# Four edits to a decoder layer's small products: the value sums' turn, the new tokens' scores, the running sums and the inner norms

## The chip, the cores and the metric

The kernel runs on one core of one Trainium2 chip. A core has TensorE (PE: matrix products, with weights loaded by a second queue, PEld), VectorE (DVE), ScalarE (ACT), GpSimd (POOL) and SyncE (SP), which issues most of the transfers. Every engine takes its instructions in the order of its own list and waits for the others on semaphores. SBUF is the working memory with 128 partitions, PSUM holds the results of products in eight banks. The metric is the device time of one execution in microseconds (us).

## The reference

One step of a decoder with one layer on two groups of tokens at once: a prompt of 256 tokens, and 8 sequences of 4 new tokens each (32 tokens) with a past of 1024 tokens in pages of 128 rows. All inputs are float32.

```python
hp = ffn_half(hp, norm_ffn1, w_ffn1_gate, w_ffn1_up, w_ffn1_down)   # h + 1/2 * (silu(n@wg) * (n@wu)) @ wd
cb, u, q, k, v, logf = mixer_in(hp, norm_mix, w_in, b_f)             # one projection, log sigmoid of 8 gates
conv_y = cb * short_conv(u_ext, conv_w)
attn_o = fox_prompt(q, k, v, logf)        # new tokens: fox_sample(..., cache_k, cache_v, cache_logf, page_table)
hp = mixer_out(hp, conv_y, attn_o, norm_conv_out, norm_attn_out, w_out)  # each group normalised by itself
hp = ffn_half(hp, norm_ffn2, ...)
hp = ple_add(hp, p_prompt, norm_ple, w_ple_gate, w_ple_proj)
y_prompt = rms_norm(hp, norm_final)
```

and for the new tokens

```python
F = jnp.cumsum(lf_all, axis=1).transpose(0, 2, 1)       # running sum of log forget values, past and new
s = jnp.einsum('bqhd,bkhd->bhqk', q, k_all) * SCALE
s = s + Fq[..., None] - F[:, :, None, :]                # Fq: the running sums at the new tokens
s = jnp.where(kpos <= qpos, s, -jnp.inf)
return jnp.einsum('bhqk,bkhd->bqhd', jax.nn.softmax(s, axis=-1), v_all)
```

`rms_norm(x, g)` is `x * rsqrt(mean(x*x) + 1e-6) * g`. D_MODEL is 2048, D_FF 5632, there are 8 heads of 128, and the page table says which pages of the pool a sequence has.

## The kernel before

Everything is held with features on the partitions and the 288 tokens (256 prompt, 32 new) in the free dimension: `h` is 128 x 16 x 288. Weights come as float32 pieces of 512 by 256 (`wraw`, 512 KB). For accuracy each operand is split into a high part in float32r and the rest: `whi` (ACT, line 271) and `wlo` (DVE, line 272) of the weights, `xh` and `xl` of the activations. Three products give one: `whi*xh`, `whi*xl`, `wlo*xh` (lines 304 to 306). `pair` (line 282) makes two output blocks of 128 features of such products; a piece of weights is a chunk of it, 4 k-tiles x 2 blocks x 3 = 24 products, and its splits are made up to five half pieces ahead (`HALVES`).

The program is one list of steps that is written out in order: first feed-forward, mixer, second feed-forward, per-layer embedding, final norm. Small work goes between the chunks in two ways. `defer(fn, n)` (line 334) puts a function off by n chunks; `run_deferred` calls what is due in the middle of a chunk, after its first block's 12 products. In the mixer, `at(i, ...)` (line 952) puts functions ahead of the i-th chunk of the filling work, and functions at one mark run in the order in which they were added. From this list the framework plans each engine's own order when the kernel is built, by its estimate of when operands are ready, with the order of the program as priority; a few instructions are pinned (`keep_in_program_order`).

What the change touches:

- **Inner norms.** The squares of `h` are added up over the 16 k-tiles in `acc` (line 209). `norm_scale` (line 190) defers `inv_rms` (line 175) by 1 to 3 chunks. That sums over the partitions by a product of the 128 x 128 constant `mean` (1/2048 everywhere) with the squares, in float32 (line 180), then makes the inverse root with two activations on ACT and three operations on DVE. It is called six times: at the eighth chunk for the first norm (line 444, two chunks), at the end of each feed-forward (line 397, three), for the convolution's group (line 999, two), the attention's group (line 1000, one), and at the end of the mixer (line 1006, three). The final norm calls `inv_rms` by itself (line 1066).
- **Running sums.** `f_past` (line 530) scans the log forget values of the 64 pages and keeps each page's total per head in `tot` (64 x 8). `f_natural` (line 555) turns those of the new tokens to rows (`nat`, columns 32 to 40). `f_new`, `f_turn` and `f_rows` (lines 566 to 595), each a chunk after the one before, add up totals and new values per new token by two products (lines 568, 569), turn the result (line 576), spread it over the 128 rows of (head, sequence, half, token) by a product (line 583), and make from it the bias `newbias` of the new tokens' scores and the running sum at each query, `Fq`.
- **New tokens' scores.** The keys of the past come by 16 key units (`k_scores`, line 667), one at every third mark from 1, each 16 products in column tiles of 32 (line 684). Eight units make the scores of four sequences, a group. `new_scores` (line 695) makes the scores among the new tokens of a group, 16 short products in the same column tiles (line 699), at marks 20 and 21; `softmax(0)` is at mark 27.
- **Value sums.** `v_round` (line 733) takes a page of values of each of the four sequences; after the eighth round `sample_out` (line 750) takes the heads' diagonal blocks out of PSUM into `so`, eight operations of DVE (lines 762 and 764), and defers `sample_turn` (line 767) by two chunks, which turns `so` (line 770) and puts it into `oS` (line 772). The second group's turn then stores the values and normalises. The first group's `sample_out` is at mark 69, as is the first of the eight `prompt_head` calls (line 784); two of the chunks behind carry the gated convolution's evacuations (line 848).

Of the kernel before, what the change touches and what calls it, by code (L numbers as in the profile page):

```python
# [16 lines left out]
F32 = mybir.dt.float32  # L17
F32R = mybir.dt.float32r
I32 = mybir.dt.int32
AF = mybir.ActivationFunctionType  # L20
ALU = mybir.AluOpType
# [4 lines left out]
P = 128  # L26
D = 2048
# [3 lines left out]
DT = 4  # L31
NS = DB * DT
NT = SEQ + NS
DFF = 5632
NH = 8
# [26 lines left out]
def constants():  # L62

    rows = np.arange(P)
    hc, b, half, t = rows // 32, rows % 32 // 8, rows % 8 // 4, rows % 4
    h = 4 * half + hc
    parts = []

    def put(name, a):
        a = np.asarray(a, np.float32)  # L70
        full = np.zeros((P, a.shape[1]), np.float32)
        full[: a.shape[0]] = a
        at = sum(x.shape[1] for x in parts)
        CONST_COLS[name] = (a.shape[0], at, at + a.shape[1])
        parts.append(full)

    put("ident", np.eye(P))
    put("ones", np.ones((P, 1)))
    put("mean", np.full((P, P), 1.0 / D))
    put("iota", rows[:, None])  # L80
    put("headmask", (rows % 8 // 4 * 4 + rows % 32 // 8)[:, None] == np.arange(NH)[None])
    put("tri", np.where(np.arange(P)[None] <= rows[:, None], 0.0, NEG))
    cb, ct = np.arange(NS) // DT, np.arange(NS) % DT
    for g in range(2):
        own = (cb[None] == (b + 4 * g)[:, None])
        put(f"newmask{g}", np.where(own & (ct[None] <= t[:, None]), 0.0, NEG))
        put(f"newself{g}", own & (ct[None] == t[:, None]))
    put("fold", rows[:, None] % 32 == np.arange(NH)[None])
    put("tri32", (cb[:, None] == cb[None]) & (ct[:, None] <= ct[None]))
    pb, pg = np.arange(64) // PAGES, np.arange(64) % PAGES  # L90
    put("tri64", (pb[:, None] == pb[None]) & (pg[:, None] < pg[None]))
    put("sel64", pb[:, None] == cb[None])
    put("headsel", np.arange(NH)[:, None] == h[None])
    return np.concatenate(parts, 1)


def build(nc, tc, ctx, A, O):
# [3 lines left out]
    v, s, g, pe, sy = nc.vector, nc.scalar, nc.gpsimd, nc.tensor, nc.sync  # L101

    cst = pool("cst")
# [14 lines left out]
    def ktbank():  # L118

        names = [n for n in spare["tags"] for _ in range(BANKS[n])]  # L120
        spare["at"] += 1
        n = names[spare["at"] % len(names)]
        return bank(n, BANKS[n])
# [3 lines left out]
    h = cst.tile([P, KT, NT], F32, name="h")  # L127

    def const(name):
        r, a, b = CONST_COLS[name]  # L130
        return C[:r, a:b]

    ident = const("ident")
# [5 lines left out]
    at = 0  # L139
# [32 lines left out]
    def log_tables():  # L172
        tc.keep_in_program_order(s.preload_act_table_set("natural_log_exp_and_others"))

    def inv_rms(out, parts, width, load=True):

        b = ktbank()
        m = b[:, :NT]
        for i, x in enumerate(parts):
            pe.matmul(m, const("mean"), x, start=i == 0, stop=i == len(parts) - 1)  # L180
        if load:
            log_tables()
        c = float(D // width)
        s.activation(ra, m, AF.Ln, bias=eps, scale=c)
        s.activation(out, ra, AF.Exp, scale=-0.5)
        v.scalar_tensor_tensor(ra, out, -0.5 * c, out, ALU.mult, ALU.mult)
        v.scalar_tensor_tensor(ra, m, EPS / c, ra, ALU.add, ALU.mult)
        v.scalar_tensor_tensor(out, ra, 1.5, out, ALU.add, ALU.mult)

    def norm_scale(out, squares, width, chunks):  # L190

        defer(lambda: inv_rms(out, [squares], width), chunks)

    def split(hi, lo, x, gcol):
        return (s.activation(hi, x, AF.Copy, scale=gcol),
# [138 lines left out]
    def defer(fn, chunks=1):  # L334

        deferred.append((state["chunk"] + chunks, fn))
# [218 lines left out]
    def f_natural(lf, FT):  # L555
        fp = W["fp"][0]
        np_ = ktbank()
        nat = cst.tile([P, 40], F32, name="nat")
        for j in range(2):
            pe.transpose(np_[:, 16 + j * NH:16 + j * NH + NH], FT[:, j * P:j * P + P], ident[:NH, :NH])  # L560
        pe.transpose(np_[:NS, 32:40], lf[:, SEQ:], ident[:NH, :NH])
        v.tensor_copy(nat[:, 16:32], np_[:, 16:32])
        v.tensor_copy(nat[:NS, 32:40], np_[:NS, 32:40])
        M["nat"] = nat

        def f_new():
            pn = ktbank()
            pe.matmul(pn[:NS, :NH], const("tri32"), nat[:NS, 32:40], start=True, stop=False)
            pe.matmul(pn[:NS, :NH], const("sel64"), M["tot"], start=False, stop=True)
            Fn = fp.tile([NS, NH], F32, name="Fn")  # L570
            v.tensor_copy(Fn, pn[:NS, :NH])
            defer(lambda: f_turn(Fn))

        def f_turn(Fn):
            pt = ktbank()
            pe.transpose(pt[:NH, :NS], Fn, ident[:NS, :NS])
            FnT = fp.tile([NH, NS], F32, name="FnT")
            v.tensor_copy(FnT, pt[:NH, :NS])
            defer(lambda: f_rows(FnT))

        def f_rows(FnT):
            px = ktbank()
            pe.matmul(px[:, :NS], const("headsel"), FnT, start=True, stop=True)
            Fx = fp.tile([P, NS], F32, name="Fx")
            v.tensor_copy(Fx, px[:, :NS])
            M["newbias"], M["Fq"] = [], []
            for gi in range(2):
                nb = cst.tile([P, NS], F32, name=f"nbias{gi}")
                v.tensor_tensor(nb, const(f"newmask{gi}"), Fx, ALU.subtract)
                d = fp.tile([P, NS], F32, name=f"fd{gi}")  # L590
                v.tensor_tensor(d, Fx, const(f"newself{gi}"), ALU.mult)
                fq = cst.tile([P, 1], F32, name=f"fq{gi}")
                v.tensor_reduce(fq, d, AX.X, ALU.add)
                M["newbias"].append(nb)
                M["Fq"].append(fq)

        defer(f_new)
# [97 lines left out]
    def new_scores(gi):  # L695
        sc = ktbank()
        for half in range(2):
            for c in range(4):
                pe.matmul(sc[32 * c:32 * c + 32, :NS], M["qn"][gi][:, 4 * half + c, :], k_[4 * half + c][:, SEQ:],
                          start=half == 0, stop=half == 1, tile_position=(0, 32 * c))  # L700
        v.scalar_tensor_tensor(M["s", gi][:, PAGES * P:], sc[:, :NS], M["Fq"][gi], M["newbias"][gi], ALU.add, ALU.add)
# [48 lines left out]
    def sample_out(gi):  # L750
        mx = W["vv"][0]
        for b in range(4):
            for e in range(2):
                rows = slice(NS * e, NS * e + NS)
                pe.matmul(M["va", gi][e][32 * b:32 * b + 32, :], M["pv", gi][rows, 8, b], M["vs"][rows], start=False, stop=True,
                          tile_position=(NS * e, 32 * b))
        o = mx.tile([P, P], F32, name="so", tag="so", bufs=2)
        for hh in range(NH):
            src = M["va", gi][hh // 4][:, hh % 4 * P:hh % 4 * P + P]
            m = const("headmask")[:, hh:hh + 1]  # L760
            if hh == 0:
                v.tensor_scalar(o, src, m, None, ALU.mult)
            else:
                v.scalar_tensor_tensor(o, src, m, o, ALU.mult, ALU.add)
        defer(lambda: sample_turn(gi, o), 2)

    def sample_turn(gi, o):
        mx = W["vv"][0]
        t = ktbank()
        pe.transpose(t[:, :P], o, ident)  # L770
        for half in range(2):
            v.tensor_copy(M["oS"][:, 4 * half:4 * half + 4, 16 * gi:16 * gi + 16].rearrange("p c (b t) -> p c b t", t=DT),
                          t[:, :P].rearrange("p (b c a t) -> p a c b t", c=4, a=2, t=DT)[:, half])
        if gi == 1:
            s.dma_start(O["v_prompt"].rearrange("(j p) c -> p j c", p=P), M["vn"])
            for e in range(2):
                s.dma_start(O["v_sample"][:, 512 * e:512 * e + 512], M["vs"][NS * e:NS * e + NS])
            for hh in range(NH):
                split(za[hh][0][:, SEQ:], za[hh][1][:, SEQ:], M["oS"][:, hh, :], gain("norm_attn_out", hh))
            sq = mx.tile([P, NH, NS], F32, name="sqS")  # L780
            s.activation(sq, M["oS"], AF.Square)
            v.tensor_reduce(acc[:, SEQ:], sq.rearrange("p h n -> p n h"), AX.X, ALU.add)
# [169 lines left out]
    def at(i, *fns):  # L952
        marks.setdefault(i, []).extend(fns)
# [31 lines left out]
        fill += pair(A["w_out"], ob * 256, list(range(8)), lambda k: zc[k], out_conv(ob), late=1 if ob == 0 else 0)  # L985
    for n in range(16):
        at(1 + KSTEP * n, units[n] if n > 1 else units[n][1])
    at(20, lambda: new_scores(0))
    at(21, lambda: new_scores(1))
    at(27, lambda: softmax(0))  # L990
    at(49, lambda: softmax(1))
    at(48, v_start)
# [144 lines left out]
```

## Time and profile before

| | |
|---|---|
| median of 3 runs | 2333.52 us (2333.39 to 2333.70) |
| span of the profiled execution, first to last instruction | 2332.0 us |
| time of the profiled execution itself | not listed apart from the three; the runs lie 1.4 to 1.7 us above the span |
| mean granted TensorE clock | 0.998 |
| busy: PE, PEld, DVE, ACT, POOL | 99%, 97%, 57%, 45%, 14% of the span |
| read from and written to HBM | 435.56 MB, 5.07 MB |

How to read the rows: in a group of instructions (a line that begins with a line number) stand the line, the engine, the operation, output <- inputs, shapes and the number of instructions, then busy time and mean ns of one, then the idle time of the engine just before them and what ended it. In a timeline stand the start and the duration in us, the engine, the line, the operation, the tiles, how many were merged, and in brackets an idle time of the engine before it. In the chain of waits stand a start, a length, and what the time went to. A product in float32 appears as two instructions (x2), one in float32r as one. In the view of waits stand the waiting instruction, what it waited for, the total in us, the number and the longest.

### The profile page before, as it was taken

The page shows a single profiled execution, that of the slowest core. Times are in us where ns is not written, and L with a number is a line of the kernel's source. Part 1 is how long each engine was busy: PE and PEld are TensorE (multiplying, and loading weights), DVE is VectorE, ACT ScalarE, POOL GpSimd, SP SyncE. Part 2 cuts the span into 40 slices and gives each one's busy share as a digit, 9 for nine tenths or more (in the row PEclk, how much of TensorE's full clock was granted, in tenths as well). Part 3 has the DMA queues.
Part 4 walks back from the last instruction along what each step waited for, and adds up shares of the span by engine and source line. Part 5 has one row for each costly group of instructions (what it writes and reads, how often), then busy time and mean ns, then how long its engine had stood idle before and what let it go on. Part 6 is the DMA issues. An engine that isn't in the chain of part 4 may idle for free.

```text
span 2332.0 us, 44271 instructions
## 1 busy us (share of the span) xinstructions
PE 2316.4 (99%) x17390; PEld 2254.6 (97%) x17390; DVE 1338.6 (57%) x2395; ACT 1056.0 (45%) x1859; POOL 328.2 (14%) x401
## 2 busy tenths in 40 slices
PE   9999999999999999999999999999999999999997
PEld 9999999999999999888888999999999999999997
DVE  6555555555555575456466765555555555555755
ACT  7444444444444453334345554444434444444654
POOL 2010000000000013444445210000000000000110
PEclk9999999999999999999999999999999999999999
DMA  8575555545555457998988554545555555555452
GB/s 272 162 241 163 165 169 164 164 164 167 167 163 163 163 161 224 333 313 268 322 306 296 167 165 154 174 158 175 163 164 164 170 163 163 164 167 167 161 169 88
DMA packets 391137, 443.52 MB, mean 190 GB/s; under 512 B 17120, under 2 KB 371824, under 8 KB 390928
## 3 DMA queue, kind: packets, MB, share of 16 engines
q1 hardware_dynamic: 369456, 366.89, 49.3%
q0 software_dynamic: 20384, 71.38, 8.8%
q8 instruction: 136, 2.23, 0.4%
q10 hardware_dynamic: 1088, 2.42, 0.3%
q14 instruction: 73, 0.60, 0.1%
HBM read 435.56 MB, written 5.07 MB: 189 GB/s over the span
## 4 chain that ended last, share of the span: by engine, by line
PE 99%; DVE 0%; DMA 0%; ACT 0%; SPq 0%; issue 0%; DVEq 0%
PE mm L304 31%; PE mm L306 31%; PE mm L305 30%; PE va L742 1%; PE va L684 1%; PE va L304 1%; PE va L306 1%; PE va L305 1%; DMA h<-in_x_dram 0%; DVE h L1072 0%; PE kt L304 0%; PE kt L306 0%; PE kt L305 0%; PE kt L180 0%; PE kt L796 0%; PE kt L829 0%
## 5 line engine op out<-in xcount | busy, mean ns | idle before, releaser
L272 DVE TENSOR_TENSOR wlo<-wraw,whi 128x512 fp32r<-128x512 f32 x1384 | 972.0, 706 | 805.2 <-ACT whi L271 753.2
L271 ACT ACTIVATE whi<-wraw 128x512 fp32r<-128x512 f32 x1384 | 865.3, 630 | 938.5 <-PE mm L305 866.0
L304 PE MATMUL mm<-xh,whi 128*128 128x288 f32 x3680 | 1094.9, 298 | 0.0
L305 PE MATMUL mm<-xl,whi 128*128 128x288 f32 x3680 | 1085.6, 295 | 0.0
L306 PE MATMUL mm<-xh,wlo 128*128 128x288 f32 x3680 | 1082.0, 294 | 0.0
L304 PEld LDWEIGHTS mm<-xh,whi 128*128 128x128 f32 x3680 | 689.7, 187 | 23.2 <-issue 19.4
L306 PEld LDWEIGHTS mm<-xh,wlo 128*128 128x128 f32 x3680 | 692.9, 188 | 0.1
L305 PEld LDWEIGHTS mm<-xl,whi 128*128 128x128 f32 x3680 | 691.0, 188 | 0.2
L304 PE MATMUL mm<-hh,whi 128*128 128x288 f32 x1408 | 416.8, 296 | 0.0
L305 PE MATMUL mm<-hl,whi 128*128 128x288 f32 x1408 | 415.4, 295 | 0.0
L306 PE MATMUL mm<-hh,wlo 128*128 128x288 f32 x1408 | 414.0, 294 | 0.0
L370 POOL TENSOR_TENSOR sr<-sg,rs 128x288 f32<-128x288 f32 x88 | 72.3, 822 | 1409.2 <-ACT sg L368 1409.1
L306 PEld LDWEIGHTS mm<-hh,wlo 128*128 128x128 f32 x1408 | 265.2, 188 | 0.0
L305 PEld LDWEIGHTS mm<-hl,whi 128*128 128x128 f32 x1408 | 264.4, 188 | 0.0
L304 PEld LDWEIGHTS mm<-hh,whi 128*128 128x128 f32 x1408 | 263.8, 187 | 0.0
L390 DVE SCALAR_TENSOR_TENSOR h<-mm,h 128x288 f32<-128x288 f32 x192 | 87.1, 455 | 23.4 <-PE mm L306 23.0
L215 POOL TENSOR_TENSOR acc<-acc,sq 128x288 f32<-128x288 f32 x59 | 51.0, 865 | 248.5 <-ACT sq L214 245.6
L368 ACT ACTIVATE sg<-tg 128x288 f32<-128x288 f32 x88 | 39.1, 444 | 99.9 <-DVE tg L366 96.7
L243 POOL DMA_INDIRECT KT<-in_cache_k_dram,idx x64 | 65.0, 1015 | 122.9 <-PE va L684 54.6
L377 ACT ACTIVATE hh<-hd 128x288 fp32r<-128x288 f32 x88 | 39.2, 446 | 92.8 <-DVE hd L375 92.8
L247 POOL DMA_INDIRECT page<-in_cache_v_dram,idx x64 | 64.7, 1010 | 72.6 <-PE va L742 50.6
L378 DVE TENSOR_TENSOR hl<-hd,hh 128x288 fp32r<-128x288 f32 x88 | 40.7, 464 | 22.0 <-ACT hh L377 22.0
(231 smaller groups left out, 1319.4 us busy)
## 6 DMA issues: line engine op xcount, KB each, us to landing
wraw<-in_w_ffn_up_dram SPq DMA_DIRECT2D x176, 512.0 KB
wraw<-in_w_ffn_gate_dram SPq DMA_DIRECT2D x175, 512.0 KB
wraw<-in_w_ffn_down_dram SPq DMA_DIRECT2D x160, 512.0 KB
wraw<-in_w_in_dram SPq DMA_DIRECT2D x96, 512.0 KB
wraw<-in_w_out_dram SPq DMA_DIRECT2D x32, 512.0 KB
wraw<-in_w_ple_gate_dram SPq DMA_DIRECT2D x32, 512.0 KB
wraw<-in_w_ffn_down_dram SPq DMA_DIRECT2D x32, 256.0 KB
wraw<-in_w_ple_proj_dram SPq DMA_DIRECT2D x8, 256.0 KB
```

What stands on the lines that cost most here:

```text
L215: (v if k >= KT - last_on_v else g).tensor_tensor(acc, acc, sq, ALU.add)
L243: g.indirect_dma_start(out=t[:, i].rearrange("p h s -> p (h s)"), out_offset=None, in_=it["src"], in_offset=bass.IndirectOffsetOnAxis(ap=r ...
L247: g.indirect_dma_start(out=t, out_offset=None, in_=it["src"], in_offset=bass.IndirectOffsetOnAxis(ap=it["rows"], axis=0))
L271: s.activation(hi, x, AF.Copy)
L272: v.tensor_tensor(lo, x, hi.bitcast(F32), ALU.subtract)
L304: pe.matmul(o, hi[:, j % 2, w], xh, start=f, stop=False)
L305: pe.matmul(o, hi[:, j % 2, w], xl, start=False, stop=False)
L306: pe.matmul(o, lo[:, j % 2, w], xh, start=False, stop=l)
L370: g.tensor_tensor(r, u, rs, ALU.mult)
L377: s.activation(H["hi"][:, k, :], t, AF.Copy)
L378: v.tensor_tensor(H["lo"][:, k, :], t, H["hi"][:, k, :].bitcast(F32), ALU.subtract)
L390: v.scalar_tensor_tensor(h[:, k, :], o, 0.5, h[:, k, :], ALU.mult, ALU.add)
```

## The change

1. **Inner norms.** GpSimd fills one column with 1/2048 and copies it out to a 128 x 128 matrix in float32r (`meanr`). `norm_scale` splits the squares at once, on ACT (`sqh`) and DVE (`sql`), and the deferred `inv_rms` sums both parts with `meanr` in two float32r products. The final norm keeps the float32 constant.
2. **Running sums.** One 96 x 128 operand `E` is laid out on DVE in `f_natural`: rows 0 to 63 have the page totals, rows 64 to 95 the new tokens' values, both repeated over the 128 columns of (head, sequence, half, token). One float32 product with the constant `newsum` (96 x 32: which total or value counts for which new token) replaces the three products and the transpose. The bias and `Fq` are made as before, two chunks earlier. The constants `tri32`, `sel64` and `headsel` go.
3. **New tokens' scores.** Both `new_scores` calls go to mark 22, where the eighth key unit (n = 7, mark 1 + 3 * 7) stands; they were added after it and so run behind it.
4. **Value sums.** The first group's `sample_turn` is deferred by 4 chunks instead of 2.

```diff
-    put("tri32", (cb[:, None] == cb[None]) & (ct[:, None] <= ct[None]))
...
-    put("sel64", pb[:, None] == cb[None])
-    put("headsel", np.arange(NH)[:, None] == h[None])
+    put("newsum", np.concatenate([pb[:, None] == cb[None], (cb[:, None] == cb[None]) & (ct[:, None] <= ct[None])]))
...
+    meanr = cst.tile([P, P], F32R, name="meanr")
+    mean1 = cst.tile([P, 1], F32, name="mean1")
+    g.memset(mean1, 1.0 / D)
+    g.tensor_copy(meanr, mean1.to_broadcast([P, P]))
+    sqh, sql = (cst.tile([P, NT], F32R, name=f"sq{x}") for x in "hl")
+
-    def inv_rms(out, parts, width, load=True):
+    def inv_rms(out, parts, width, load=True, weights=const("mean")):
...
-            pe.matmul(m, const("mean"), x, start=i == 0, stop=i == len(parts) - 1)
+            pe.matmul(m, weights, x, start=i == 0, stop=i == len(parts) - 1)
...
     def norm_scale(out, squares, width, chunks):
 
-        defer(lambda: inv_rms(out, [squares], width), chunks)
+        s.activation(sqh, squares, AF.Copy)
+        v.tensor_tensor(sql, squares, sqh.bitcast(F32), ALU.subtract)
+        defer(lambda: inv_rms(out, [sqh, sql], width, weights=meanr), chunks)
...
+        def spread(rows, src):
+
+            for a in range(2):
+                v.tensor_copy(E[rows].rearrange("p (c b a t) -> p c b a t", c=4, b=4, a=2)[:, :, :, a],
+                              src[:, 4 * a:4 * a + 4].unsqueeze(2).unsqueeze(3).to_broadcast([src.shape[0], 4, 4, DT]))
+
+        E = fp.tile([96, P], F32, name="sums")
+        spread(slice(0, 64), M["tot"])
+        spread(slice(64, 96), nat[:NS, 32:40])
+
         def f_new():
-            pn = ktbank()
-            pe.matmul(pn[:NS, :NH], const("tri32"), nat[:NS, 32:40], start=True, stop=False)
-            pe.matmul(pn[:NS, :NH], const("sel64"), M["tot"], start=False, stop=True)
...
-            pe.transpose(pt[:NH, :NS], Fn, ident[:NS, :NS])
...
             px = ktbank()
-            pe.matmul(px[:, :NS], const("headsel"), FnT, start=True, stop=True)
+            pe.matmul(px[:, :NS], E, const("newsum"), start=True, stop=True)
...
-        defer(lambda: sample_turn(gi, o), 2)
+        defer(lambda: sample_turn(gi, o), 4 if gi == 0 else 2)
...
-    at(20, lambda: new_scores(0))
-    at(21, lambda: new_scores(1))
+    at(22, lambda: new_scores(0), lambda: new_scores(1))
```

More of the change, by code (lines that the diff above doesn't have):

```diff
@@ L64, in constants @@
     rows = np.arange(P)
-    hc, b, half, t = rows // 32, rows % 32 // 8, rows % 8 // 4, rows % 4
-    h = 4 * half + hc
+    b, t = rows % 32 // 8, rows % 4
     parts = []
@@ L564, in f_natural @@
         M["nat"] = nat
-        def f_new():
-            pn = ktbank()
[L568 to L581, printed above, removed]
+        def spread(rows, src):
[5 more added lines that the diff above has]
+        spread(slice(64, 96), nat[:NS, 32:40])
+        def f_new():
             px = ktbank()
-            pe.matmul(px[:, :NS], const("headsel"), FnT, start=True, stop=True)
+            pe.matmul(px[:, :NS], E, const("newsum"), start=True, stop=True)
             Fx = fp.tile([P, NS], F32, name="Fx")
```

## The prediction

> **What bounds the kernel now.** I read the page first (share of each engine, the chain that ended last), then the list of waits for TensorE (PE) alone, then the chain of waits in order of time around each place that the change touches, then the timelines of ScalarE (ACT) and VectorE (DVE) at those places. From the page:
>
> ```profile
> span 2332.0 us, 44271 instructions
> PE 2316.4 (99%) x17390; PEld 2254.6 (97%) x17390; DVE 1338.6 (57%) x2395; ACT 1056.0 (45%) x1859; POOL 328.2 (14%) x401
> PE 99%; DVE 0%; DMA 0%; ACT 0%; SPq 0%; issue 0%; DVEq 0%
> L271 ACT ACTIVATE whi<-wraw 128x512 fp32r<-128x512 f32 x1384 | 865.3, 630 | 938.5 <-PE mm L305 866.0 <-PE mm L306 29.1 <-PE va L305 10.8
> ```
>
> The reader is to see that the chain is PE nearly alone, and that the other engines wait for PE and not PE for them: of the 938.5 us that ACT sits idle before a weight split, 866.0 end when a product releases a split buffer. So a microsecond saved on DVE, ACT, GpSimd (POOL) or a DMA is worth nothing, and one saved in PE's own stream is worth one. The waits of PE of half a microsecond and more, from the view of waits:
>
> ```profile
> PE mm L461 <- DVE acc L458: 1.3, 1, 1.3
> PE kt L770 <- DVE pst L812: 1.3, 1, 1.3
> PE kt L180 <- ACT sq L1054: 0.7, 1, 0.7
> ```
>
> Line 461 is the start and the wait of line 180 is in `finish`; the change touches neither. It touches line 770. The rest of the question is what the four edits take out of PE's stream, and whether they put a wait in. The sum is made against the profiled execution: 2332.0 us of span, and the median of the three runs, 2333.5, lies 1.5 above that. I carry the difference of the span over to the median.
>
> **The norms.** In the chain of waits an ordinary product of the weight stream stands with 0.13. An inner norm stands like this, the first and the last but one of the six that `norm_scale` makes:
>
> ```profile
> 37.54 0.48 PE kt L180 x2
> ...
> 1364.31 0.48 PE kt L180 x2
> ```
>
> A norm's sum in float32 takes 0.48 on the path. After the change it is two products of a float32r square (`sqh`, `sql`), 288 columns wide and with 128 columns of weights, which is the very form of the stream, 0.13 each: 0.27 together. Six times 0.48 - 0.27 = 0.21 is **1.26 us**. The final norm keeps `mean` in float32. Above, that is the bound, since a pair of products can't be cheaper than two of its neighbours; below, should something that this trace doesn't show slow the pair, it is the 0.48 of today again and no gain. I take the neighbours' price because operands, shapes and types are theirs.
>
> Each of the six gets two more instructions ahead of it, a copy on ACT and a subtraction on DVE. The nearest rows:
>
> ```profile
> L377 ACT ACTIVATE hh<-hd 128x288 fp32r<-128x288 f32 x88 | 39.2, 446 | 92.8 <-DVE hd L375 92.8
> L378 DVE TENSOR_TENSOR hl<-hd,hh 128x288 fp32r<-128x288 f32 x88 | 40.7, 464 | 22.0 <-ACT hh L377 22.0
> ```
>
> so 0.45 + 0.46 = 0.91 and, with two handoffs, about 1.0 us between the last addition into `acc` and the second product. Where is that much room? The first norm is the tight one; ACT, then DVE:
>
> ```profile
> 35.86 1.66 ACT L271 ACTIVATE whi<-wraw 128x512 fp32r<-128x512 f32 x3
> 35.93 1.01 DVE L215 TENSOR_TENSOR acc<-acc,sq 128x288 f32<-128x288 f32 x2
> 36.86 1.89 DVE L272 TENSOR_TENSOR wlo<-wraw,whi 128x512 fp32r<-128x512 f32 x3
> ```
>
> `acc` is done at 35.93 + 1.01 = 36.94. A product starts 0.16 ahead of its piece in the chain (1364.15 in the timeline below, 1364.31 above), so PE came to the norm at 37.38: the cover was 0.44. With the pair, `sql` is ready at 37.95 at best, while PE reaches the second product at 37.51: a new wait of **0.4 us**. If instead `sqh` stands behind the three splits on ACT (35.86 + 1.66 = 37.52) and `sql` behind the three on DVE (36.86 + 1.89 = 38.75), it is ready at 39.2 and PE waits 1.7. If the planner of the build sees the lateness and gives PE other products first, the wait is 0. I take 0.4, which is nearest to the rows when the pair goes ahead of the splits, as it does in the order of the program. At the next tightest,
>
> ```profile
> 1361.45 0.45 DVE L215 TENSOR_TENSOR acc<-acc,sq 128x288 f32<-128x288 f32 x1
> 1364.15 0.65 PE L180 MATMUL kt<-acc,consts 128*128 128x288 f32 x2
> ```
>
> 2.25 us lie between 1361.90 and the product, more than twice the 1.0; I charge nothing there, and the cover is that gap.
>
> GpSimd's two new instructions, a fill and a broadcast, stand with its other fills at the start, and nobody needs the matrix before the first norm at 37 us, which is their cover. The constants are 160 columns narrower, and no wait of PE above is for their transfer. Both 0.
>
> **The running sums.** Three visits of PE go (the pair L568 and L569, the transpose L576, the spread L583) and one comes. In the chain the price of a visit is its own piece and what the product behind it has over 0.13. The three visits, in order:
>
> ```profile
> 887.24 0.15 PE kt L568 x2
> 887.39 0.15 PE kt L569 x2
> 887.54 0.33 PE mm L304
> ```
>
> ```profile
> 890.93 0.12 PE kt L576
> 891.05 0.33 PE mm L304
> ```
>
> ```profile
> 894.45 0.33 PE kt L583 x2
> 894.78 0.33 PE mm L304
> ```
>
> and, for the new product, two float32 products on the whole array and what follows them:
>
> ```profile
> 1194.30 0.22 PE kt L795 x2
> 1194.52 0.43 PE kt L796 x2
> 1194.96 0.13 PE mm L304
> ```
>
> The three cost 0.15 + 0.15 + 0.20 = 0.50, 0.12 + 0.20 = 0.32 and 0.33 + 0.20 = 0.53: 1.35 us. The new product has 96 rows, 128 columns of weights and 32 moving columns. Above, L583's 0.53 bounds it (the same weights' width and moving columns, on 8 rows); below, L795's 0.22 (whole array, 128 moving columns, and 0.13 behind it). I take 0.33: L583's own piece without the 0.20, because the whole-array rows pay nothing behind them. Gain 1.35 - 0.33 = **1.02**, ends 0.82 and 1.13. By the Trainium skill, TensorEngine Tiling, Key Properties, changing the tiling mode drains the array; the 0.33 behind L568, L576 and L583 against 0.13 behind L796 agrees, and since its list of modes has none of 96 rows, the new product would pay no drain, so 0.33; with a drain the sum would be 0.20 smaller. DVE loses two small copies out of PSUM and gets four small ones one chunk before the product; a chunk is 24 products, 24 x 0.13 = 3.2 us, and that is their cover.
>
> **The new tokens' scores.** Two visits of L699, of which the first is shown, and ahead of it a key unit (L684) like the one that both now follow:
>
> ```profile
> 982.46 1.85 PE va L684 x16
> 984.31 0.33 PE mm L304
> ...
> 987.70 0.26 PE kt L699 x16
> 987.96 0.33 PE mm L304
> ```
>
> If the second is like the first, apart they cost 2 x (0.26 + 0.20) = 0.92. Behind the unit, whose tiles have the same shape and which pays its own 0.20, the two 0.20 go for sure, and some of the 0.26, which holds the entry. Gain between 0.40 and 0.60; I take **0.50**. The writes into the score rows come two chunks and one chunk later, and the first softmax stands five chunks behind. No DMA goes with them.
>
> **The value sums.** The one wait of PE inside the kernel, as the chain has it, and the same turn of the second group:
>
> ```profile
> 1191.31 0.55 DVE wlo L272
> 1191.86 0.06 issue
> 1191.92 0.34 DVE so L764
> ```
>
> ```profile
> 1293.39 0.11 PE kt L770
> ```
>
> and PE's timeline:
>
> ```profile
> 1190.85 0.29 PE L306 MATMUL mm<-xh,wlo 128*128 128x288 f32 x1
> 1192.41 0.30 PE L770 MATMUL kt<-consts,so 128*128 128x128 f32 x1 [1.26 <-DVE pst L812]
> ```
>
> The last of the eight sums into `so` stood in DVE's queue behind a split of weights, which ended late itself: 1191.92 + 0.34 = 1192.26, while PE came by at 1190.98. From 1190.85 to 1192.41 are 1.56, where 0.13 would do; the same turn of the second group costs 0.11. Two chunks later (over 6 us) `so` is long done, so **1.43 us** go. The turn issues no DMA (only that of the second group does); its two copies on DVE come behind the second head's scores, the gated convolution's evacuations and a round of values, and who reads them, the turn of the second group, is 100 us away. Next in line to be late is the first head's transpose (L820), which now comes 1.4 earlier:
>
> ```profile
> 1192.92 0.54 DVE L814 TENSOR_SCALAR px<-px,pst 128x128 f32<-128x128 f32 x2
> 1196.39 0.49 PE L820 MATMUL kt<-consts,px 128*128 128x128 f32 x3
> ```
>
> Its rows are ready at 1193.46, it would start at about 1194.96: 1.5 to spare.
>
> **The sum.** 1.26 + 1.02 + 0.50 + 1.43 = 4.21 less 0.4 for the first norm is 3.8: the span falls to 2328.2, the median to **2329.7 us**, 0.16%. About 0.2% (4.7 us) is what a measurement of this kernel tells from no change, so a correct forecast here reads as no change.
>
> **The rivals.** *More than counted* (2328.8): the scores hide wholly under the unit's last tiles (0.92 for 0.50), the new sum costs 0.22, the planner avoids the first wait: 1.26 + 1.13 + 0.92 + 1.43 = 4.74. Against it: L684 to the next product takes 0.33, so the array is not free while the unit ends. *The wait only moves* (2331.1): DVE is as late for L820 or a later reader as it was for `so`, and the 1.43 come back: 4.21 - 1.43 - 0.4 = 2.4. For it: DVE is in order and behind splits there; against it: the 1.5 to spare. *The late pair at the first norm alone* (2331.0): 4.21 - 1.7 = 2.5; for it, the splits in a row there, against it, that the pair stands ahead of them in the program. *Slower* (2339.5): the pair stands behind the splits on ACT and DVE at all six norms, not only at the first, and PE, in order, waits 1.7 each time: 10.2 - 4.2 = +6.0. It evens out at 0.7 per norm and reads as slower from 1.5 per norm. For it: 1.66 of splits on ACT and 1.89 on DVE stood in a row at the first norm; against it: the 2.25 at the next tightest. By the Trainium skill, TensorE: Matmul & The Clock Gate, Part 1, on the depths of the engines' queues, ACT and DVE are strictly first in, first out and only weight loads overtake on PE, so nothing could step around such a queue; `so` behind the split at 1191.31 agrees.
>
> **How the numbers follow.** Forecast (2329.0 to 2330.5) 0.53; late first norm 0.14; the wait moves 0.09; more than counted 0.13; slower 0.08; other ways inside 0.2% 0.03. Range: below, the case of more than counted with 0.2 for the spread of the runs, 2328.6; above, the wait moved and a late first norm together, 4.21 - 1.43 - 1.7 = 1.1, or 2332.4, and up to the point where it all comes to half a microsecond, 2333.0. That leaves out the slower case and part of the last one. Faster by over 0.2% is the more-than-counted case and a little of the forecast's own lower edge, 0.15; slower 0.08; the rest, 0.77, within.
>
> **What would show it.** Each step right: the chain has the inner norms as two pieces of 0.13; one visit of about 0.33 with 0.13 behind it in place of L568, L576 and L583; both scores in one stay behind the eighth key unit with one 0.33; the first L770 at 0.11 and gone from PE's waits; at most a wait of 0.4 at the first norm. Wrong: a PE wait for `sql` over 1 us, a wait of PE for DVE at L820 or L829, 0.33 behind the new sum, or a float32r norm piece over 0.13.

## The result, and the profile after

The changed kernel takes 2329.72 us (median of 18 runs, 2329.11 to 2330.52) where the kernel before, run beside it, takes 2333.61 (18 runs, 2333.18 to 2334.04): a ratio of 0.9984, 95% interval 0.9977 to 0.9990, or 3.9 us. The forecast was 2329.7 and within 0.2%. That agreement hangs on where it was run, as the experiments show: one of the four terms, the largest, was there in some sets of runs and not in others. (A set is a group of kernels that were timed together. There are four: that of this result, whose chip isn't recorded, and three of experiments, on three different chips. Below they are the first to the fourth set.)

Line numbers are those of each kernel's own text, so added lines shift them: the weight splits L271 and L272 of the kernel before are L276 and L277 in the changed kernel, and the three products of the weight stream (L304 to L306) are L309 to L311.

The page of the changed kernel, its first two lines:

```profile
span 2327.8 us, 44281 instructions
PE 2313.8 (99%) x17385; PEld 2253.9 (97%) x17385; DVE 1341.0 (58%) x2403; ACT 1058.0 (45%) x1865; POOL 330.5 (14%) x403
```

PE's busy time fell by 2.6 us and DVE's, ACT's and POOL's rose by about 2 each: work went from the engine that sets the end to three that don't. The other 1.6 of the 4.2 us of span is less idle time of PE. The waits of PE of over half a microsecond, after (what waited, on whom, us in total, times, longest):

```profile
PE mm L466 <- DVE acc L463: 1.3, 1, 1.3
PE kt L183 <- ACT sq L1053: 0.7, 1, 0.7
```

These are the start and `finish`; the wait of the first turn (L770) is gone, and no new one over half a microsecond has come. The chain of waits of the changed kernel at the first norm, at the second, at the sums and at the scores (start, us, what; `...` marks rows left out):

```profile
37.41 0.13 PE kt L183
37.54 0.01 issue
37.55 0.40 PE kt L183
...
860.34 0.27 PE kt L183 x2
...
886.97 0.14 PE kt L583 x2
887.12 0.21 PE mm L309
...
992.72 1.85 PE va L684 x16
994.57 0.30 PE kt L699 x29
994.87 0.33 PE mm L309
```

The second norm is two products of 0.13, as forecast; the first holds a wait, for `sql` on DVE, which the product that reads it follows at once (DVE, then PE):

```profile
37.04 0.45 DVE L196 TENSOR_TENSOR sql<-acc,sqh 128x288 fp32r<-128x288 f32 x1
37.55 0.40 PE L183 MATMUL kt<-sql,meanr 128*128 128x288 f32 x1
```

The sum's one product takes 0.14, and the product behind it 0.21, not 0.33. Both scores together stand behind the key unit (L684) for 0.30, with one 0.33. And PE's timeline at the first turn:

```profile
1198.37 0.30 PE L311 MATMUL mm<-xh,wlo 128*128 128x288 f32 x1
1198.50 0.27 PE L770 MATMUL kt<-consts,so 128*128 128x128 f32 x1
1198.61 0.59 PE L829 MATMUL kt<-pT,vn 128*128 128x256 f32 x2
```

The turn starts 0.13 behind the product ahead of it, and in one stay with the first head's value products.

For the terms I take a stricter measure than the chain's pieces: from the start of the last product of the weight stream ahead of a place to that of the fifth behind it, less 0.133 for each of the products. By it the norms cost 0.47 each before and 0.26 after (the first 0.54); the sums 0.51 + 0.32 + 0.53 = 1.35 before and 0.22 after; the scores 0.46 + 0.46 apart before and 0.29 behind the unit; the first turn 1.56 before, 0.11 after. That is 1.0 + 1.13 + 0.63 + 1.45 = 4.2, the difference of the two spans.

### The profile page after: what moved, and what is told of

Read it like the earlier page. It is cut to its first block, busy times and chain, and to the rows that moved or that the text cites. A ratio compares the mean times of both kernels' runs of the same rounds, so it can differ in the third digit from the quotient of the medians.

```text
span 2327.8 us, 44281 instructions
## 1 busy us (share of the span) xinstructions
PE 2313.8 (99%) x17385; PEld 2253.9 (97%) x17385; DVE 1341.0 (58%) x2403; ACT 1058.0 (45%) x1865; POOL 330.5 (14%) x403
## 4 chain that ended last, share of the span: by engine, by line
PE 99%; DVE 0%; ACT 0%; issue 0%; DVEq 0%
PE mm L309 31%; PE mm L311 31%; PE mm L310 31%; PE va L742 1%; PE va L684 1%; PE va L309 1%; PE va L311 1%; PE va L310 1%; PE mm L466 0%; DVE h L1071 0%; PE kt L311 0%; PE kt L309 0%; PE kt L310 0%; PE kt L796 0%; PE kt L829 0%; PE kt L183 0%
## 5 line engine op out<-in xcount | busy, mean ns | idle before, releaser
L277 DVE TENSOR_TENSOR wlo<-wraw,whi 128x512 fp32r<-128x512 f32 x1384 | 972.6, 706 | 801.1 <-ACT whi L276 744.7
L276 ACT ACTIVATE whi<-wraw 128x512 fp32r<-128x512 f32 x1384 | 865.9, 630 | 932.0 <-PE mm L310 863.7
L309 PE MATMUL mm<-xh,whi 128*128 128x288 f32 x3680 | 1094.3, 297 | 0.0
L311 PE MATMUL mm<-xh,wlo 128*128 128x288 f32 x3680 | 1081.9, 294 | 0.0
L309 PEld LDWEIGHTS mm<-xh,whi 128*128 128x128 f32 x3680 | 689.7, 187 | 22.2 <-issue 17.7
L311 PEld LDWEIGHTS mm<-xh,wlo 128*128 128x128 f32 x3680 | 693.0, 188 | 0.1
L309 PE MATMUL mm<-hh,whi 128*128 128x288 f32 x1408 | 416.8, 296 | 0.0
L311 PE MATMUL mm<-hh,wlo 128*128 128x288 f32 x1408 | 414.0, 294 | 0.0
L311 PEld LDWEIGHTS mm<-hh,wlo 128*128 128x128 f32 x1408 | 265.2, 188 | 0.0
L309 PEld LDWEIGHTS mm<-hh,whi 128*128 128x128 f32 x1408 | 263.8, 187 | 0.0
```

The source lines that it names most:

```text
L276: s.activation(hi, x, AF.Copy)
L277: v.tensor_tensor(lo, x, hi.bitcast(F32), ALU.subtract)
L309: pe.matmul(o, hi[:, j % 2, w], xh, start=f, stop=False)
L311: pe.matmul(o, lo[:, j % 2, w], xh, start=False, stop=l)
```

## The experiments

**One part at a time.** Each of the four edits alone in the kernel before, timed on one chip with 33 runs of the kernel before beside them (the second set). The norms:

```diff
...
-        defer(lambda: inv_rms(out, [squares], width), chunks)
+        s.activation(sqh, squares, AF.Copy)
+        v.tensor_tensor(sql, squares, sqh.bitcast(F32), ALU.subtract)
+        defer(lambda: inv_rms(out, [sqh, sql], width, weights=meanr), chunks)
```

> The kernel before with the inner norms alone changed (float32r pair, matrix from GpSimd). Terms of the prediction: six norms save 1.26 us, the first gives 0.4 back as a wait for sql, so the span falls by 0.86, to 2331.1. Read from the trace of the changed kernel (five norms at 0.26 where 0.47 stood, the first at 0.54): by 0.98, to 2331.0. Rival, that the pair is no cheaper on the path and the fall of the changed kernel came from elsewhere: 0 within 0.2. Rival, that the wait at the first norm came from the other edits: a fall of 1.25 and no wait there.

The sums:

```diff
-            pe.matmul(pn[:NS, :NH], const("tri32"), nat[:NS, 32:40], start=True, stop=False)
-            pe.matmul(pn[:NS, :NH], const("sel64"), M["tot"], start=False, stop=True)
...
-            pe.matmul(px[:, :NS], const("headsel"), FnT, start=True, stop=True)
+            pe.matmul(px[:, :NS], E, const("newsum"), start=True, stop=True)
```

> The kernel before with the running sums alone in one product of 96 rows. Term of the prediction: the span falls by 1.02 us, to 2331.0 (the new product costs 0.33 on the path). Read from the trace of the changed kernel (three visits of 1.35, now 0.22): by 1.13, to 2330.9. Rival, that a product of 96 rows is a change of mode with a drain: the piece behind it is 0.33 again and the fall is 0.82. Rival, that the four small copies on VectorE cost PE a wait: less than 0.5.

The scores:

```diff
-    at(20, lambda: new_scores(0))
-    at(21, lambda: new_scores(1))
+    at(22, lambda: new_scores(0), lambda: new_scores(1))
```

> The kernel before with the new tokens' scores alone moved behind the eighth key unit. Term of the prediction: the span falls by 0.50 us (0.40 to 0.60), to 2331.5. Read from the trace of the changed kernel (two visits of 0.46 apart, now 0.29 for both behind the unit): by 0.63, to 2331.4. Rival, wholly hidden under the unit: 0.92, to 2331.1. Rival, that their later writes make the first softmax late: no fall.

The turn:

```diff
-        defer(lambda: sample_turn(gi, o), 2)
+        defer(lambda: sample_turn(gi, o), 4 if gi == 0 else 2)
```

> The kernel before with the first group's turn alone made four chunks behind its sums instead of two. Term of the prediction: the span falls by 1.43 us, to 2330.6, and no wait of PE for VectorE stands between 1185 and 1200 us. Rival, the wait only moves to the first head's transpose or a later reader: 0 to 0.3 fall, and a wait of PE for VectorE over 1 us at that reader.

Here the kernel before took 2332.14 us, 1.5 less than in the first set. Medians of 11 runs: norms 2331.29 (-0.85), sums 2330.93 (-1.21), scores 2331.52 (-0.62), turn 2332.18 (+0.04). The interval of each ratio is 0.0009 to either side, 2 us, and holds 1 for all four; the sizes therefore rest on the traces, where the same three places cost what they cost in the changed kernel: five norms 0.26, the sum 0.22, both scores 0.29. But the first norm of the kernel with the norms alone cost 0.89, so that this traced run gained about 0.64 by its norms. Its time, 2331.68, lies above the median of 2331.29.

The turn alone brought nothing. And the three kernels that keep the turn at two pieces had no wait there: in each the turn cost about 0.1. The view of PE's waits for the kernel with the norms alone has the two rows as above and no third (the wait at the first norm is too small for that list; its price shows it). So the question was whether the wait belongs to the kernel or to the set of runs.

**Does the wait belong to the kernel? Does a write make it?** In the prediction the last sum stood behind a weight split "which ended late itself"; I had not asked why. My first theory was a late transfer: 8 us ahead of the turn ACT issues a write of 1 MB (L775). Four kernels, the third set: the kernel before once more, unchanged;

> The kernel before, unchanged, for a second trace of it. Of four kernels with one part each, the three that keep the first turn two pieces behind its sums showed no wait there either (1.45 us less at that place), and the kernel with the turn alone moved was no faster than the kernel before beside it. Theory: the wait of 1.3 us is not a fixture; it comes when a piece of weights lands late, and a trace with a span near 2330.5 has no wait of PE at the first turn, one near 2332 has it. Rival: the kernel before always has it, and the three kernels lost it through their own edits; then the span is 2331.7 to 2332.3 with the wait in the trace.

the write put off to the second turn (issued at 1291.1 us, where it was 1182.7);

```diff
-            s.dma_start(O["v_prompt"].rearrange("(j p) c -> p j c", p=P), M["vn"])
+            tc.keep_in_program_order(s.dma_start(O["v_prompt"].rearrange("(j p) c -> p j c", p=P), M["vn"]))
```

> The kernel before with the write of the values of the prompt (1 MB, issued at 1182.7, some 8 us ahead of the first turn) kept behind the second turn, at about 1293. Theory, the late weights at the turn come from this write beside them: ACT's split ahead of the last sum starts by 1189.2, PE does not wait at the turn, and the span is 1.2 to 1.5 less than that of the kernel before if that one has the wait, the same within 0.2 if not. Rival, the gathers of value pages make them late: the wait is as in the kernel before.

the write made twice;

```diff
+    VD = drp.tile([SEQ, NH * P], F32, name="VD")
...
             s.dma_start(O["v_prompt"].rearrange("(j p) c -> p j c", p=P), M["vn"])
+            s.dma_start(VD.rearrange("(j p) c -> p j c", p=P), M["vn"])
```

> The kernel before with the same write of 1 MB made twice, the second into a scratch of its own, right behind the first. Theory, the write makes the weights late and the late weights make the last sum late: PE waits at the first turn, 1.3 us or more, and the span is at least 1.2 above that of the kernel with the late write. Rival, the weights' lateness has nothing to do with the write: no more wait than in the kernel before, difference within 0.3.

and the same two lines added to the changed kernel.

> The changed kernel with the same write made twice. Theory, the turn two chunks later stands behind the late sum: no wait of PE at the first turn, where the kernel before with the double write has one, and the two kernels with double writes differ by 4.0 or more, of which 2.7 are the norms, sums and scores. Rival, the wait moves on: PE waits over 0.5 us for VectorE at the first head's transpose or at the turn, and the difference is 3 or less.

Here the kernel before took 2333.53 (33 runs, none under 2333.1) and unchanged again 2333.66, with the wait in its trace (1.1). With the write gone from there, the wait stayed at 1.1, and the time was 2333.93. With two writes the wait was gone: 2331.95, 1.58 less; by the stricter measure its turn cost 0.10, against 1.43 in the unchanged kernel of this set. The theory of the write is wrong, in both directions. What took the wait away with two writes is an order: with one more instruction on ACT, the plan of the build has the last sums ahead of the split. VectorE in that kernel (L765 is the sum that was L764):

```profile
1188.84 1.11 DVE L765 SCALAR_TENSOR_TENSOR so<-va,consts,so 128x128 f32<-128x128 f32 x3
1189.86 0.15 DVE L814 RECIPROCAL pst<-pst 128x2 f32<-128x2 f32 x1
1190.05 0.83 DVE L816 TENSOR_SCALAR px<-px,pst 128x128 f32<-128x128 f32 x2
1190.89 1.29 DVE L272 TENSOR_TENSOR wlo<-wraw,whi 128x512 fp32r<-128x512 f32 x2
```

All three sums run in a row and the split comes a microsecond later. That is a cleaner look at the cause than the kernel was made for: it is the one sum behind the split that PE waits for. The changed kernel with two writes (2329.92) has the same order, so it tells nothing of where a late sum's wait would go; its waits of PE at the turn and at the first head's transpose are nil. It is 2.03 faster than the kernel before with two writes, where 4.0 or more was expected: the turn has nothing left to give there, and the first norm cost 1.12 in its trace, against 0.54 in the changed kernel's.

**Where the lateness comes from.** The chain of the kernel before in the first set, from just ahead of the rows that the prediction shows:

```profile
1189.28 0.13 PE mm L305
1189.42 1.24 PE mm L306
1190.66 0.62 ACT whi L271
```

One product of the stream has 1.24 in place of 0.13. PE itself did not stop; its timeline shows a product each 0.13 there. What is late is the word that products are done. ACT's split waits for a free buffer, so for products of PE to be complete. In the traces, the updates of PE's semaphore for four products stand like this (starts of the products, then the updates):

```
kernel before, first set      1188.32 1188.45 1189.12 1189.25 -> 1190.56 1190.59 1190.66 1190.69
norms alone, second set       1188.47 1188.61 1189.27 1189.40 -> 1188.78 1188.91 1189.58 1189.71
```

In the second row each update comes 0.31 behind its product's start. In the first, four come in one bunch, up to 2.2 us behind. ACT at that place, first in the kernel before, then in the norms alone (where L811 is L819 and L271 is L279):

```profile
1189.03 0.18 ACT L811 ACTIVATION_READ_ACCUMULATOR px<-px,pst 128x1 f32 x1
1190.64 0.63 ACT L271 ACTIVATE whi<-wraw 128x512 fp32r<-128x512 f32 x1 [1.42 <-PE mm L306]
```

```profile
1188.73 0.19 ACT L819 ACTIVATION_READ_ACCUMULATOR px<-px,pst 128x1 f32 x1
1188.86 0.63 ACT L279 ACTIVATE whi<-wraw 128x512 fp32r<-128x512 f32 x1
```

The split starts 1.4 us after ACT is free in the one, at once in the other; then DVE's split follows it, then the last sum, then PE. All six traces of the first and the third set have this bunch at this place, the changed kernel's too; none of the eight traces of the second and the fourth has one anywhere. Of the some 3,000 products of the stream's form with an update in an execution, each of the six traces has 65 to 80 whose update is missing or over 0.52 us behind the start (the first products of the program, before 20 us, left out). All of them lie between 129 and 139 us or between 918 and 1271 us; GpSimd issues the gathers of cache pages from 127 to 140 us and, with pauses, from 913 to 1270 us. TensorE is not alone in this: in the same six traces, at 127 to 140 us and at 917 to 1270 us, 43 to 48 of some 2,320 updates of VectorE and 20 to 31 of some 1,830 of ScalarE are missing or over 0.3 us behind the end of their instruction, where 0.01 is usual, and in the other eight traces there are none of these. What holds the updates back, and why in these sets, stays open; no run here changes the gathers.

**The turn back at two pieces.** The fourth set. The changed kernel unchanged, and with the turn as before:

> The changed kernel, unchanged, for a trace and times beside the next three. Theory: where the kernel before has its wait of 1.3 us at the first turn (times near 2333.5), the changed kernel is 3.9 faster; where it has not (times near 2332.1), 2.7 faster, which is the sum of norms, sums and scores as they were measured alone (0.85 + 1.21 + 0.62). Rival: 3.9 on either chip.

```diff
-        defer(lambda: sample_turn(gi, o), 4 if gi == 0 else 2)
+        defer(lambda: sample_turn(gi, o), 2)
```

> The changed kernel with the first turn back at two pieces behind its sums. Theory, the turn's wait hangs on late completions of TensorE's products, which some chips show and others do not: 1.2 to 1.5 slower than the changed kernel with a wait of PE at the turn, if the kernel before has that wait on this chip, and the same within 0.2, with no wait, if not. Rival, the other three parts have moved the place so that the sums are in time anyway: no wait and no difference, also where the kernel before has the wait.

The kernel before took 2332.20 here (33 runs), so this was a chip like that of the second set. The changed kernel took 2329.64, ratio 0.9988 (0.9979 to 0.9997): 2.56 us, which is the sum of the three parts alone (2.68) and not 3.9. With the turn back at two pieces it was 2329.64 again. Its DVE and PE there:

```profile
1187.20 0.73 DVE L764 SCALAR_TENSOR_TENSOR so<-va,consts,so 128x128 f32<-128x128 f32 x2
1187.85 0.88 DVE L277 TENSOR_TENSOR wlo<-wraw,whi 128x512 fp32r<-128x512 f32 x1
1188.65 0.34 DVE L764 SCALAR_TENSOR_TENSOR so<-va,consts,so 128x128 f32<-128x128 f32 x1
```

```profile
1189.45 0.27 PE L770 MATMUL kt<-consts,so 128*128 128x128 f32 x1
1189.48 0.38 PE L309 MATMUL mm<-xh,whi 128*128 128x288 f32 x1
```

The last sum is still behind the split, but the split is in time, and the sum ends at 1188.99, 0.46 ahead of the turn. In the changed kernel of the first set the same three stand so:

```profile
1187.25 0.73 DVE L764 SCALAR_TENSOR_TENSOR so<-va,consts,so 128x128 f32<-128x128 f32 x2
1189.31 0.69 DVE L277 TENSOR_TENSOR wlo<-wraw,whi 128x512 fp32r<-128x512 f32 x1 [1.33 <-ACT whi L276]
1189.92 0.35 DVE L764 SCALAR_TENSOR_TENSOR so<-va,consts,so 128x128 f32<-128x128 f32 x1
```

There the sum ends at 1190.27, while PE passes the old place of the turn at 1189.08. The lateness is still there; the later turn steps around it, and about 1.2 us is what the turn at two pieces would have waited by these rows. That is an estimate: no run has the changed kernel with the turn at two pieces in a set that shows the bunches. The kernel before was not traced in the second and the fourth set; that it has no wait there is read from its times and from the four kernels that share its order at the turn.

**The first norm three pieces behind.** The fourth set too:

```diff
             if c == 7:
-                norm_scale(rs, acc, D, 2)
+                norm_scale(rs, acc, D, 3)
```

> The changed kernel with the first inner norm three chunks behind its squares instead of two. Theory, the pair of products comes 24 products (3.2 us) later, long behind sql: the norm costs 0.26 like the other five, and the span is 0.3 to 0.9 less than that of the changed kernel, which paid 0.54 at that norm on one chip and, with the norms alone, 1.1 on another. Rival, the scale is then late for the evacuation of the first gate and up products: a new wait of PE of 0.3 us or more near 42 us, and no gain.

The chain at that norm, and the one new piece behind it:

```profile
40.54 0.27 PE kt L183 x2
...
47.60 0.45 PE mm L309 x2
```

The norm's wait is gone, and 0.16 came back as a hesitation seven microseconds later. The time is 2329.73 against 2329.64: no gain that can be measured. The traced run was at the short end of its 11 (span 2327.6, median 2328.0); the changed kernel's median span there was 2327.9. Where the trace's 0.3 goes in the other runs isn't settled. No version was found that beats the changed kernel.

**64 rows, and the scores together but away from the unit.** The fourth set. With 64 rows the kernel leaves the new tokens' own log forget values out of the running sums:

```diff
-            pe.matmul(px[:, :NS], E, const("newsum"), start=True, stop=True)
+            pe.matmul(px[:, :NS], E[:64], const("newsum")[:64], start=True, stop=True)
...
-    at(22, lambda: new_scores(0), lambda: new_scores(1))
+    at(20, lambda: new_scores(0), lambda: new_scores(1))
```

> The changed kernel with two places altered. The sum's product has 64 rows in place of 96, so the new tokens' own log gates are left out of the running sums; and both new tokens' scores stand together two chunks ahead of the key unit, not behind it. Sum: theory, 64 rows are another mode of the array than 128, and the visit costs 0.5 with 0.33 behind it; rival, as with 96 rows, 0.22 and nothing behind. Scores: theory, what is saved is the second entry and exit and, behind the unit, the first too, so both together away from the unit cost 0.60 to 0.65, against 0.92 apart and 0.29 behind the unit; rival, only the joining counts, about 0.3. In all 0.6 slower than the changed kernel by the theory, 0 by the rivals.

The chain at both places:

```profile
886.95 0.34 PE kt L583 x2
887.29 0.33 PE mm L309
...
986.61 0.39 PE kt L699 x32
987.00 0.33 PE mm L309
```

With 64 rows the sum takes 0.34 and has 0.33 behind it, where 96 rows took 0.14 and 0.21: 0.53 against 0.22 by the stricter measure, the price of the old spread with 8 rows. Fewer rows made it dearer by 0.31. The scores together but apart from the unit cost 0.59, between the 0.92 apart and the 0.29 behind the unit: the joining is worth 0.33 and the unit 0.30. Both theories came out in the trace, 0.61 in all; the time rose by 0.54 (2330.18), less than the interval of the timing (0.0009 of a ratio to either side), so the two sizes rest on the trace.

## Why the prediction was right, and where not

**The bound.** Right: PE's stream set the end, and what left it left the time. The difference of span, 4.2, is the sum of four local differences in that stream.

**The norms**, 1.26 forecast: right for five of the six, 0.21 each.

**The wait at the first norm**, 0.4 forecast between 0 and 1.7: right in kind and about the middle of what was found. The pair did go ahead of all but one split, and in all six traces that have it at two pieces the next product of the stream starts 0.29 behind the end of `sql`. `sql` ended between 37.50 and 37.91 us, and PE came by earlier or later, so that the wait was 0.16 to 0.86 (0.27 in the changed kernel's first trace). The two rival forms, a pair behind all splits (1.7) and such a wait at all six (+6.0), didn't come: at the other five nothing waits.

**The sums**, 1.02 forecast within 0.82 to 1.13: the mechanism was right and the term mis-sized. I had taken the new product at L583's own piece, 0.33, when it is 0.22, the price of L795, which I had named as the lower bound. L583's 0.33 was itself a part of the price of its 8 rows, as the run with 64 rows shows. The Trainium skill, TensorEngine Tiling, Key Properties, says that a change of the tiling mode drains the array; the 0.33 behind 64 rows against 0.21 behind 96 agrees, and the 0.34 against 0.14 ahead shows that the change costs at the entry too.

**The scores**, 0.50 forecast within 0.40 to 0.60: 0.63, just over the range. The entry was saved too, more than the part of it that I had allowed.

**The turn**, 1.43 forecast: 1.45 in the first set, and nothing in two of four. The chain of the one trace did show the wait, and its removal does remove it; the step that failed is the unsaid one, that a wait seen in one execution is a fixture of the kernel. The prediction named its last link (a split that "ended late itself") and didn't follow it one link further, to the 1.24 at L306. Even so the rival that the wait moves on was rightly held unlikely: L820 waits for nobody.

**The sum.** 3.8 forecast and 3.9 measured in the first set; beside the 2.56 of the fourth the same forecast would have been 1.2 too much. The result was timed in the same set as the three runs listed ahead of the prediction (they are the first three of its 18), so the wait was there to be removed. The prediction gave no reason why it would be, and to that extent the agreement is luck. Two terms too small by 0.11 and 0.13 and a wait of 0.27 in place of 0.4, all to the same side, are the span's 4.2 against 3.8. The prediction also held that a change under 0.2% reads as no change; the first set's interval, 0.9977 to 0.9990, leaves 1 out.

## What to carry to other kernels

Before a wait of the trace is priced, follow it to the link that is not explained by its engine's own work, here a 1.24 in a row of 0.13, and ask whether another execution has it: times of the kernel before that sat 1.4 us apart from set to set said more than any one trace. In this kernel a visit of a small product to the full stream was priced by its form and not by its work: it paid to fill it up to the form of its neighbours (0.22 with 96 rows against 0.53 with 64) or to put it behind a unit of the same tiles (0.29 against 0.59), even with more arithmetic. Work put ahead of a deferred product is free only where the deferral covers its two handoffs at the tightest place, not on average.

## What was not expected of the hardware

In the traces of two of four sets of runs, completions of TensorE's products reached the other engines late and in bunches, at the first turn up to 2.2 us behind the products' start where 0.31 was usual, always in the stretches with page gathers; updates of VectorE and ScalarE were late there too. In the traces of the other two sets none was. The kernel before is 1.3 to 1.5 us slower in the sets with the bunches (2333.61 and 2333.53 against 2332.14 and 2332.20), the changed kernel is not (2329.72 against 2329.64). A float32 product of 64 rows cost PE's stream 0.53, one of 96 rows, with more in it, 0.22.
